# Swapping the order of the first two groups of projected columns in a two-stream hybrid kernel

## The chip, the cores and the metric

The kernel runs on one core of a Trainium2 chip, as one program. The metric is the device time of one execution in microseconds (us).

## The reference

The input is one sequence of 1024 tokens of width 1024, all in float32. Two layers run, each a mixer and an MLP, with RMS norms ahead and residual sums behind:

- Layer 0's mixer projects the normed input to 2560 columns (`h @ w_in`). The first 1792 are shifted (each token mixed with the one before it) and feed eight recurrent heads of 64 (RWKV-7: a state of 64 x 64 per head, updated for every token from r, k, v, a decay and a rate); the other 768 are queries, keys and values of a sliding-window attention. Both results side by side are projected by `w_out`.
- Layer 1's mixer is a gated projection, a causal depthwise convolution of 31 taps, a layer norm, SiLU and a projection.
- The MLP is `square(relu(h @ w1)) @ w2` with 4096 hidden columns.

## The kernel before

The tokens are taken in two halves of 512. Activations lie transposed, 128 columns of the model across the partitions and 512 tokens along them. Each product is made from three matmuls (`mm3`, lines 308 to 310), since both operands are split into a high part and a remainder (`lo`, line 272); weights are loaded in two pieces by SyncE's queue (line 286), cast by ScalarE (line 291), and their remainder is made by VectorE or GpSimd in turn, by a running count.

Layer 0's recurrent heads are worked on in four pairs p = 0 to 3, for each of the two halves `hf`: eight scans (`scan`, lines 571 to 869), each a chunked form of the recurrence with many small matmuls that alternate with vector work. A scan needs the three columns r, k and v of its pair (`rkv(p)` gives their indices, k and v first), which `proj` multiplies out (`w_in_tile`) and shifts (`shift`, `shifted`, lines 545 to 568; the first vector product of a column of half 0 is line 551). It begins on TensorE with the two products of lines 589 and 591, after an activation on k (line 596), and ends with the transposes of line 866 and the vector product of line 869. For half 0 the columns of pairs 0 and 1 stay on the chip; their buffers have the tags krv0 and krv1, by the parity of the column. The columns of pairs 2 and 3 and of half 1 go to memory and are loaded again (lines 945 and 950).

The scans form two streams, A and B, each a serial chain:

```python
def scans_b():
    yield from first1()
    yield from self.scans(1, [(0, 0), (0, 2)])
    self.close(self.cms1)
    self.done.add("b")
...
gs = {"p": params, "A": lambda: self.scans(0, [(0, 1), (0, 3), (1, 0), (1, 1), (1, 2), (1, 3)]), "B": scans_b,
      "n": self.norm0, "0": lambda: att(0), "1": lambda: att(1)}
self.weave(main(), *[gs[c]() for c in ORDER])
```

A pair in the lists is (half, p). A, the longer one, has six scans, B two. B first normalizes and stores the second half (`first1`, transposes of line 355), and its working memory is that of this step.

TensorE's order of instructions is written by a planner (`weave`) when the program is built: it keeps a clock that adds a planned time for TensorE work alone, and takes steps in turn from a base line, `main`, and from the other generators. Each generator names at its `yield` either a planned time after which it is due again (the constants in `LAG`) or a flag that it waits for (`self.done`). Of several due generators the first in `ORDER = "1BAn0p"` is taken, so attention's second part, then B, then A; a ratio limits how much they take from main. The other engines' order is made by the framework from the dependences.

Main is: `cols0` (the columns of half 0; it raises the flags "lg", "0p0" to "0p3" and the attention's), `cols1` (those of half 1), then, behind the flag "b", the output projection of half 0 (`w_out`, which casts the mixers' results in line 1168 and needs the flags "s2", "s3" and "att0" for its parts), the last columns of half 1 and the first half of layer 0's MLP. `scans` waits for "0p1" before A's first scan and for "0p0" before B's; then comes a planned time of `LAG["load"]` and one of `LAG["lora"]` ahead of the first products. Behind the weave come the second half's output projection, its MLP and layer 1.

Of the kernel before, what the change touches and what calls it, by code (L numbers as in the profile page):

```python
# [45 lines left out]
class Net:  # L46
# [1009 lines left out]
    def cols0(self, hs):  # L1056

        self.lg = []
        for j in (12, 13):
            self.lg.append((yield from self.proj(0, hs, j)))  # L1060
        self.done.add("lg")
        self.t = {}
        for p in range(2):
            self.t[p] = []
            for j in self.rkv(p):
                self.t[p].append((yield from self.proj(0, hs, j)))
            self.done.add(f"0p{p}")
        for j in (18, 19, 14, 16, 15, 17):
            yield from self.proj_att(0, hs, j)
            self.done.add(f"0k{j}")  # L1070
        for p in (2, 3):
            js = self.rkv(p)
            for j in js[:1 if p == 3 else 3]:
                yield from self.proj(0, hs, j, True)
            if p == 3:
                pss = yield from self.w_in_pair(js[1:], hs)
                for j, ps in zip(js[1:], pss):
                    self.shift(0, j, ps, True, LAG["hp"] > 0)
            self.done.add(f"0p{p}")
# [525 lines left out]
```

## Time and profile before

| | us |
|---|---|
| three runs: median (lowest, highest) | 2380.85 (2377.12, 2387.97) |
| the profiled execution, its own time | 2379.74 |
| its span, first to last instruction | 2378.0 |
| busy: TensorE / VectorE / ScalarE / GpSimd | 2308.1 / 1532.2 / 1047.7 / 542.8 |
| granted TensorE clock, mean | 0.992 |

The profile's rows give instructions by line of the kernel, with the tiles that they write and read ("out<-in"). PE is TensorE, PEld its weight loads, DVE VectorE, ACT ScalarE, POOL GpSimd, SP SyncE (SPq its queue of loads and stores). Matmuls overlap in the pipeline, so that the durations of neighbours add up to more than the time between their starts.

### The profile page before, as it was taken

To read this page: it belongs to the slowest core of one execution; us is meant where nothing else is said; L and a number is where in the kernel's file an instruction comes from. 1 tells how busy PE (TensorE), PEld (TensorE's weight loads), DVE (VectorE), ACT (ScalarE), POOL (GpSimd) and SP (SyncE) were. 2 spreads that over 40 slices of the span, in tenths; PEclk is the share of its full clock that TensorE was granted. 3 is DMA by queue.
4 is the path that set the end of the run, shared out by engine and by line. 5 is a ranking of instruction groups with operands and counts; after the bars stand their busy time and mean duration, and the time that the engine had idled before them with its cause. 6 is when DMAs were issued, how large, how long until landed. Compare 5 with 4: busy or idle time off the path is not lost.

```text
span 2378.0 us, 38508 instructions
## 1 busy us (share of the span) xinstructions
PE 2308.1 (97%) x14535; PEld 1856.4 (78%) x14535; DVE 1532.2 (64%) x2563; ACT 1047.7 (44%) x1874; POOL 542.8 (23%) x477
## 2 busy tenths in 40 slices
PE   8989889989999999999999999999999999999998
PEld 6767667767777787878888888888878778888887
DVE  7775743667555464569977653799999756533334
ACT  6546634556443332443443363534433544433333
POOL 2322433110111121322000000105555422221121
PEclk9999999999999999999999999999999999999999
DMA  7345234444445454546666665563323333433332
GB/s 219 111 110 153 83 88 132 109 127 123 136 143 178 126 175 133 169 133 200 198 195 191 194 183 172 144 188 98 98 89 98 99 93 94 129 95 98 98 97 85
DMA packets 417934, 320.12 MB, mean 135 GB/s; under 512 B 44642, under 2 KB 360276, under 8 KB 417748
## 3 DMA queue, kind: packets, MB, share of 16 engines
q1 hardware_dynamic: 413684, 309.79, 43.5%
q0 software_dynamic: 2176, 4.19, 0.6%
q10 hardware_dynamic: 1888, 3.67, 0.5%
q8 instruction: 114, 1.87, 0.3%
q14 instruction: 72, 0.59, 0.1%
HBM read 257.29 MB, written 60.29 MB: 134 GB/s over the span
## 4 chain that ended last, share of the span: by engine, by line
PE 75%; DVE 15%; DMA 4%; ACT 3%; issue 2%; SPq 0%; POOL 0%; DVEq 0%; ACTq 0%; POOLq 0%
PE mm L308 23%; PE mm L309 22%; PE mm L310 22%; DVE acc L1321 5%; DMA raw<-p 1%; PE sc L734 1%; DVE C L709 1%; DVE E L711 1%; PE sc L652 1%; DVE hidl L272 1%; PE sc L817 1%; PE sc L771 1%; DMA cx<-d 1%; DVE x L1253 1%; PE at L936 1%
## 5 line engine op out<-in xcount | busy, mean ns | idle before, releaser
L291 ACT CAST whi<-wraw 128x512 fp32r<-128x512 f32 x720 | 445.7, 621 | 986.9 <-PE mm L309 890.9
L308 PE MATMUL mm<-h,whi 128*128 128x512 f32 x1792 | 725.8, 406 | 7.1 <-ACT h L383 2.4
L310 PE MATMUL mm<-h,wlo 128*128 128x512 f32 x1792 | 704.1, 394 | 1.4 <-POOL wlo L272 1.4
L309 PE MATMUL mm<-h,whi 128*128 128x512 f32 x1792 | 703.3, 393 | 1.3 <-DVE h L272 1.0
L272 POOL TENSOR_TENSOR wlo<-wraw,whi 128x512 fp32r<-128x512 f32 x302 | 422.2, 1399 | 1233.8 <-ACT whi L291 1178.5
L1321 DVE SCALAR_TENSOR_TENSOR acc<-u,par,acc 128x512 f32<-128x512 f32 x480 | 429.8, 905 | 10.0
L308 PEld LDWEIGHTS mm<-h,whi 128*128 128x128 f32 x1792 | 339.7, 190 | 89.7 <-issue 12.8
L310 PEld LDWEIGHTS mm<-h,wlo 128*128 128x128 f32 x1792 | 339.1, 189 | 75.7 <-POOL wlo L272 2.3
L309 PEld LDWEIGHTS mm<-h,whi 128*128 128x128 f32 x1792 | 340.0, 190 | 69.0 <-issue 2.4
L308 PE MATMUL mm<-hidh,whi 128*128 128x512 f32 x992 | 389.4, 396 | 0.1
L309 PE MATMUL mm<-hidl,whi 128*128 128x512 f32 x992 | 386.0, 390 | 0.9 <-DVE hidl L272 0.9
L310 PE MATMUL mm<-hidh,wlo 128*128 128x512 f32 x992 | 384.5, 390 | 0.9 <-POOL wlo L272 0.9
L272 DVE TENSOR_TENSOR wlo<-wraw,whi 128x512 fp32r<-128x512 f32 x258 | 183.5, 712 | 200.9 <-ACT whi L291 193.2
L1253 DVE TENSOR_TENSOR x<-mm,x 128x512 f32<-128x512 f32 x248 | 166.5, 686 | 85.9 <-PE mm L310 85.5
L308 PEld LDWEIGHTS mm<-hidh,whi 128*128 128x128 f32 x992 | 186.2, 188 | 43.5 <-issue 4.2
L310 PEld LDWEIGHTS mm<-hidh,wlo 128*128 128x128 f32 x992 | 186.2, 188 | 40.3 <-POOL wlo L272 1.3
L309 PEld LDWEIGHTS mm<-hidl,whi 128*128 128x128 f32 x992 | 186.3, 188 | 40.0 <-DVE hidl L272 1.3
L272 DVE TENSOR_TENSOR hidl<-rel,hidh 128x512 fp32r<-128x512 f32 x109 | 84.9, 780 | 77.9 <-ACT hidh L1230 76.5
L1232 DVE CAST hidh<-rel 128x512 fp32r<-128x512 f32 x68 | 34.2, 506 | 89.8 <-ACT rel L1226 89.6
L1226 ACT ACTIVATE rel<-rel 128x512 f32<-128x512 f32 x128 | 80.6, 633 | 3.9 <-ACT rel L1225 0.4
L1225 ACT ACTIVATE rel<-mm 128x512 f32<-128x512 f32 x128 | 75.6, 593 | 2.2 <-DVE hidl L272 2.0
L1557 POOL COPY u<-u 128x30 f32<-128x30 f32 x8 | 3.2, 399 | 250.2 <-DVE acc L1321 250.2
(377 smaller groups left out, 2191.9 us busy)
## 6 DMA issues: line engine op xcount, KB each, us to landing
wraw<-in_mlp_w_dram SPq DMA_DIRECT2D x512, 256.0 KB
lo<-wlo SPq DMA_DIRECT2D x160, 256.0 KB
wlo<-lo SPq DMA_DIRECT2D x160, 256.0 KB
wraw<-in_cv_pw_w_dram SPq DMA_DIRECT2D x96, 256.0 KB
wraw<-in_hy_w_in_dram SPq DMA_DIRECT2D x80, 256.0 KB
wraw<-in_hy_w_out_dram SPq DMA_DIRECT2D x32, 256.0 KB
p<-stg SPq DMA_DIRECT2D x30, 256.0 KB
raw<-p SPq DMA_DIRECT2D x40, 128.0 KB
```

Source lines behind the costliest of these rows:

```text
L272: return eng.tensor_tensor(out=out, in0=x, in1=hi.bitcast(F32), op=ALU.subtract)
L291: nc.scalar.copy(out=hi, in_=raw)
L308: mm(ps, lhsT=whi, rhs=xhi, start=start, stop=False)
L309: mm(ps, lhsT=whi, rhs=xlo, start=False, stop=False)
L310: return mm(ps, lhsT=wlo, rhs=xhi, start=False, stop=stop)
L652: mm(ps[64 * q:64 * q + 64, u * P:(u + 1) * P], lhsT=src[hs, c * 64:(c + 1) * 64], rhs=ar[hs, :, c, :], start=(u == 0), stop=(u == 3), ski ...
L709: tt(out=j3[:, 0:n, 0:m], in0=a3[:, j, j + 1:16].unsqueeze(2).to_broadcast([64, n, m]), in1=x3[:, j:j + 1, 0:m].to_broadcast([64, n, m]), ...
L1225: nc.scalar.activation(out=t, in_=ps, func=AF.Relu)
L1226: nc.scalar.activation(out=t, in_=t, func=AF.Square)
L1232: nc.vector.tensor_copy(out=hi, in_=t)
L1253: last = nc.vector.tensor_tensor(out=x, in0=pss[o], in1=x, op=ALU.add)
L1321: nc.vector.scalar_tensor_tensor(out=acc, in0=u[:, j:j + H], scalar=self.pv(f"dw{j}", c), in1=acc, op0=ALU.mult, op1=ALU.add)
```

## The change

In `cols0` the loop that projects the columns of pairs 0 and 1 takes pair 1 first. The three columns of pair 1 (A's first scan) stand where those of pair 0 (B's first scan) stood, and the flags "0p1" and "0p0" are raised in this order.

```diff
@@ -1060,7 +1060,7 @@
             self.lg.append((yield from self.proj(0, hs, j)))
         self.done.add("lg")
         self.t = {}
-        for p in range(2):
+        for p in (1, 0):
             self.t[p] = []
             for j in self.rkv(p):
                 self.t[p].append((yield from self.proj(0, hs, j)))
```

## Rows read from the trace of the kernel before

**Rows 1.** The page, busy us, share of the span and instructions by engine

```profile
PE 2308.1 (97%) x14535; PEld 1856.4 (78%) x14535; DVE 1532.2 (64%) x2563; ACT 1047.7 (44%) x1874; POOL 542.8 (23%) x477
```

**Rows 2.** Stretches: from:to, length, each engine's busy us, granted clock, DMA share, GB/s

```profile
core 0: us, PE busy (x) PEld busy (x) DVE busy (x) ACT busy (x) POOL busy (x), PEclk, DMA share, GB/s
...
60.00:160.00 100.00, 86.72 (x792) 67.09 (x790) 76.38 (x190) 50.27 (x98) 29.90 (x28) 0.95 0.41 114
160.00:260.00 100.00, 97.39 (x1202) 73.02 (x1199) 65.76 (x161) 66.49 (x142) 27.64 (x41) 1.00 0.41 118
260.00:360.00 100.00, 86.48 (x1129) 66.60 (x1130) 53.05 (x135) 41.38 (x71) 39.25 (x41) 0.97 0.33 93
360.00:420.00 60.00, 60.00 (x508) 44.89 (x505) 23.43 (x45) 27.91 (x50) 21.66 (x20) 1.00 0.44 135
420.00:560.00 140.00, 131.29 (x1162) 102.04 (x1162) 97.29 (x214) 74.46 (x153) 18.52 (x16) 0.98 0.41 118
560.00:695.00 135.00, 130.84 (x1152) 102.71 (x1149) 78.68 (x193) 62.41 (x129) 19.71 (x17) 0.97 0.42 129
695.00:824.00 129.00, 128.00 (x1081) 100.09 (x1081) 72.02 (x150) 47.77 (x81) 22.27 (x19) 1.00 0.52 159
824.00:953.00 129.00, 127.52 (x1078) 100.17 (x1079) 69.60 (x151) 47.68 (x81) 20.50 (x17) 1.00 0.49 151
...
1100.00:2378.00 1278.00, 1265.41 (x5587) 1042.66 (x5585) 852.34 (x1102) 520.07 (x880) 291.35 (x208) 1.00 0.44 133
```

**Rows 3.** Timeline of PE: start, us; output projection's first, last scan's, MLP half's last product

```profile
411.31 0.40 PE L308 MATMUL mm<-mih,whi 128*128 128x512 f32 x1
...
950.84 0.60 PE L866 MATMUL sc<-ident,BD 128*128 128x128 f32 x4
...
985.77 0.39 PE L310 MATMUL mm<-hidh,wlo 128*128 128x512 f32 x1
```

**Rows 4.** Timeline of PE, first products of scans: B, A, B, A

```profile
64.26 0.69 PE L589 MATMUL sc<-lg,wa 64*128 64x512 f32 x1
...
77.53 0.69 PE L589 MATMUL sc<-lg,wa 64*128 64x512 f32 x1
...
230.25 0.69 PE L589 MATMUL sc<-lg,wa 64*128 64x512 f32 x1
...
259.90 0.69 PE L589 MATMUL sc<-lg,wa 64*128 64x512 f32 x1
```

**Rows 5.** Timeline of DVE, last vector products of the same four scans

```profile
225.46 0.68 DVE L869 TENSOR_TENSOR mi<-mi,BD 128x512 f32<-128x512 f32 x1
...
259.19 1.69 DVE L869 TENSOR_TENSOR mi<-mi,BD 128x512 f32<-128x512 f32 x1
...
379.23 0.69 DVE L869 TENSOR_TENSOR mi<-mi,BD 128x512 f32<-128x512 f32 x1
...
411.72 0.69 DVE L869 TENSOR_TENSOR mi<-mi,BD 128x512 f32<-128x512 f32 x1
```

**Rows 6.** Timeline of DVE, columns: third and sixth of pairs 0 and 1, last of pair 3

```profile
50.21 0.69 DVE L551 TENSOR_TENSOR krv<-mm,rb 128x512 f32<-128x512 f32 x1 [0.21 <-PE mm L310]
...
75.17 0.68 DVE L551 TENSOR_TENSOR krv<-mm,rb 128x512 f32<-128x512 f32 x1
...
219.22 0.68 DVE L551 TENSOR_TENSOR stg<-mm,rb 128x512 f32<-128x512 f32 x1
```

**Rows 7.** Timeline of ACT, B's first activation; in brackets idle before it and its releaser

```profile
65.19 0.72 ACT L596 ACTIVATE BD<-krv,par 128x512 f32<-128x512 f32 x1 [1.79 <-DMA hd<-xl]
```

**Rows 8.** Timeline of ACT, casts ahead of the output projection

```profile
380.01 3.75 ACT L1168 CAST mih<-mi 128x512 fp32r<-128x512 f32 x7 [0.42 <-DVE mi L869]
```

**Rows 9.** Stretches of 5 us inside the second pair of scans, columns as in rows 2

```profile
320.00:325.00 5.00, 1.20 (x31) 1.14 (x32) 1.82 (x4) 0.36 (x1) 0.79 (x1) 0.92 0.77 183
325.00:330.00 5.00, 5.00 (x18) 3.89 (x17) 0.75 (x2) 1.79 (x3) 1.21 (x1) 0.74 0.00 0
```

## Prediction

> **What bounds the kernel now.** I read the page's busy times first, then a table of stretches, then the places of the scans on TensorE in the timeline, then the waits inside the stretch that the edit touches. The page says that TensorE is busy for 97% of the span [rows 1]: what is to be seen is that it is nearly full everywhere, so an edit that neither removes nor adds TensorE work can only change its idle time or its clock. The table of stretches shows where there is any [rows 2]: from 60 to 420 us, where two scans run beside each other, TensorE is idle for 13.28 + 2.61 + 13.52 + 0 = 29.4 us, and the granted clock of 0.95 and 0.97 in two of the stretches takes another (0.05 + 0.03) x 100 = 8 us. From 420 to 695 us, one scan with the second half's attention beside it, it is 8.71 + 4.16 us idle and 0.02 x 140 + 0.03 x 135 = 6.9 us of clock. With one scan alone (695 to 953 us, two scans) only 2.5 us are idle at full clock. So all that the change can touch is a pool of about 37 us up to 420 us and 20 us behind it.
>
> Next, who waits for whom over the long run. Stream A's last scan puts its last transposes on TensorE at 950.84 us; the main line's last product of the first MLP half starts at 985.77 us [rows 3]. Main outlasts A by 35 us. Stream B's end (its last vector product, at 379.23 us) opens the output projection, whose first product starts at 411.31 us [rows 3, 5]: B has 31 us to spare there. Neither stream is the bound; main is, being TensorE itself.
>
> **The change, part by part.** Nothing is removed or added. Six columns are projected in another order; each brings the same 24 products, two weight loads of 256 KB, two casts, two remainders and the same shift work. The choice of engine for a remainder goes by a running count, so the n-th column has the same one as before, and the load queue sees loads of one size in the same places. The two streams' columns go to different buffer tags, so no buffer is reused in another order among the six. Cost of these: 0, and there is no wait in them to uncover.
>
> What moves are the flags. "0p1" rises after the third pair-column instead of the sixth, "0p0" after the sixth instead of the third. In the profile the third column's vector product starts at 50.21 us, the sixth's at 75.17 us [rows 6]. B's first scan starts at 64.26 us, A's at 77.53 us [rows 4]. B was not held by its columns (done at 50.21) but by the second half's normalization, behind which its first activation waits for the store of that half until 65.19 us [rows 7]. A was held by the sixth column. Afterwards A is ready at 50.21 us; I give it the 6 us that the planned load time and first lag take, since B's flag needs such a lag too, so A starts at 56 us: 21.5 us earlier. B takes A's place at the sixth column: 77.5 us, 13.3 us later, past the store, whose wait falls away; it was ScalarE's (1.79 us idle) and hid behind columns on TensorE, so it is worth 0. The two lags between the starts become 21.5 us (was 13.3) in the first pair.
>
> How long a scan lasts, from its first product to the end of its last vector product [rows 4, 5]: leader of the first pair 225.46 + 0.68 - 64.26 = 161.9 us; its follower 259.19 + 1.69 - 77.53 = 183.4; leader of the second pair 379.23 + 0.69 - 230.25 = 149.7; its follower 411.72 + 0.69 - 259.90 = 152.5.
>
> A afterwards: first scan 56 + 161.9 = 218 to 56 + 183.4 = 239 us. Its second needs columns of pair 3, whose last vector product comes at 219.22 us [rows 6]; with the same 6 us that is 225 us at the earliest, so it starts at 225 to 243 and ends at 375 to 396 us, 16 to 37 us earlier than now. All four later scans of A move up by about as much, and main's 35 us of lead become 50 to 70. Main still ends last: worth 0. The group that needs A's second scan in the output projection, now served at 412.4 us with nothing to spare, gets spare time; that it lacked any costs little today, since 360 to 420 us has no idle time at all [rows 2].
>
> B afterwards: first scan 77.5 + 161.9 = 239 to 261 us, second start 239 to 265 (now 4 us behind the end of the first), end 389 to 417.5 us. The output projection needs a cast (3.75 / 7 = 0.54 us [rows 8]) and a remainder behind that, so about 1.3 us: B must end by 410.0. The cost is 0 for most of this interval and 7.5 us at its end. Queued behind this flag is all of main, and A's third scan alone could fill TensorE. I take 1 us: the middle of the interval (403) is in time.
>
> The stalls of the two pairs cannot be read for offsets that did not run. The offsets were 13.3 us with 13.28 + 2.61 + 5 = 20.9 us lost, and 29.7 us with 13.52 + 3 = 16.5 us lost [rows 2, 4]. They become 21.5 and, from the ends above, about 14 to 22. Both lie between the two that ran, so both are put at the mean, 18.7: 2 x 18.7 = 37.4, as now, change 0. From below, each of the four scans could stall as little as a scan alone, 1.2 us: 4.8 instead of 37.4, a gain of 32. From above, both offsets at or under that of the first pair: 2 x 20.9 = 41.8, +4, and more only by the rival below. Behind 420 us A's third and fourth scan meet the second half's attention in another phase; of 20 us lost there I assume as much as now, with -15 to +15 for the unknown.
>
> Sum: 0 + 0 + 1 + 0 = +1 us on the profiled execution of 2379.7 us (span 2378.0 and 1.7 around it). It lies 1.1 us under the median of 2380.85, so 2382 us.
>
> One rule speaks against reading TensorE as full. The row is the 97% of [rows 1]; the weight loads of [rows 2] are busy for 251.6 of 360 us from 60 to 420 (70%) and 1042.7 of 1278 from 1100 on (82%). The Trainium skill (Perfetto Trace Analysis, Identifying the Most-Contended Engine) holds that the busy share of matmuls misjudges headroom and that the share of weight loads is the better measure. By that, up to 360 - 251.6 / 0.816 = 52 us could be had in this stretch, against 37 by idle time and clock. I stay with the idle time: the scans' weight loads are smaller ones, so that their share is lower even in a full stretch, and the edit does not create work to fill what is hidden.
>
> **The rivals.** Slower: B becomes the late one. It is now the follower in both pairs, and the follower of the first pair lost 183.4 - 161.9 = 21.5 us. For it: 320 to 330 us shows how one late step holds all of TensorE, 3.8 us idle and then a granted clock of 0.74 [rows 9]. Against it: the planner asks B ahead of A, and the second follower lost only 2.8 us. If B's first scan takes 183.4 us, its second starts at 265, and main waits for 265 + x + 1.3 - 411.3 = x - 145 us, x being its second scan. It decides from x = 157 us on (over 12 us, which is 0.5%); at x = 167, midway between the two followers, it is +22: 2403 us.
>
> Faster: the pairs interleave better. A's first scan begins in a stretch that has no idle time, and B no longer runs through the start together with it; if the first pair loses what two lone scans lose, 2.5 us instead of 20.9, that is -18: 2363 us. For it: most of the pool is there. Against it: two scans still run together with the first half's attention, whose VectorE work sets much of these waits (76 of 100 us busy from 60 to 160 [rows 2]).
>
> Nothing happens: both streams have so much to spare that only their order is swapped, and each loss is found again elsewhere: 2381 us. It is hardly to be told from the forecast and is counted with it.
>
> **How the numbers follow.** 0.5% is 12 us, about what a measurement here tells from no change. Forecast and "nothing happens" together 0.58. Slower 0.25: 0.15 by B, 0.10 by new meetings of A's later scans with the attention (+15). Faster 0.17: 0.12 by the first pair, 0.05 by the later meetings or by the headroom of the rule. The range reaches to both rivals' prices, 2362 to 2403, with about 0.09 left out on either side; the likeliest case alone has 2370 to 2393.
>
> **What would show it.** Right: first scan products at about 56 and 77.5 us, A's; A's second scan begun by 243 us and its last one ended 16 to 37 us earlier; the output projection's first product at 408 to 414 us; the end of the first MLP half within 8 us of 986; idle time from 60 to 420 us within 8 us of 29. Wrong: a stretch without main's products ahead of the output projection (B late), or over 12 us of the idle time of the pairs gone or added, or the changed order moving time behind 990 us, where I see nothing that it could reach.

## The result, and the profile after

The changed kernel takes 2397.69 us (median of six, 2392.44 to 2403.76), the kernel before 2379.36 us: a ratio of 1.0078 with a 95% interval of 1.0061 to 1.0095. It is slower by 0.8%: inside the range, but above the 2393 us to which the likeliest case alone reached. The profiled execution took 2392.44 us with a span of 2390.7 us, 12.7 us longer than before; it is the shortest of the six, so it shows the loss at its smallest.

The page's engine row of the changed kernel, to be read beside [rows 1]: the same instructions on TensorE.

```profile
PE 2317.9 (97%) x14535; PEld 1860.3 (78%) x14535; DVE 1534.2 (64%) x2563; ACT 1046.3 (44%) x1874; POOL 541.1 (23%) x477
```

Its stretches, as in [rows 2]:

```profile
60.00:160.00 100.00, 84.90 (x753) 65.50 (x753) 74.51 (x183) 46.28 (x87) 27.90 (x28) 0.91 0.41 112
160.00:260.00 100.00, 93.67 (x1101) 68.56 (x1099) 53.93 (x127) 54.44 (x114) 25.00 (x37) 0.95 0.39 115
260.00:360.00 100.00, 88.74 (x1164) 69.21 (x1164) 63.42 (x166) 50.80 (x99) 38.33 (x39) 0.95 0.33 91
360.00:420.00 60.00, 60.00 (x561) 45.10 (x561) 22.82 (x51) 26.71 (x47) 22.29 (x22) 1.00 0.37 112
420.00:560.00 140.00, 133.66 (x1131) 103.77 (x1131) 91.37 (x196) 70.48 (x143) 22.97 (x19) 0.94 0.42 123
560.00:695.00 135.00, 130.61 (x1186) 101.31 (x1185) 82.70 (x205) 66.70 (x143) 19.83 (x17) 0.99 0.43 131
```

From 60 to 420 us TensorE is idle for 15.10 + 6.33 + 11.26 + 0 = 32.7 us, 3 more than before. The column of the granted clock is what moved: 0.91, 0.95 and 0.95 take 19 us where 0.95, 1.00 and 0.97 took 8, and 420 to 560 us has 0.94 where it had 0.98.

The places of the scans and of main in the timeline of TensorE, as in [rows 3, 4]: the four first scans, the output projection's first product, the last scan's transposes, the MLP half's last product.

```profile
58.66 0.69 PE L589 MATMUL sc<-lg,wa 64*128 64x512 f32 x1
...
80.58 0.90 PE L589 MATMUL sc<-lg,wa 64*128 64x512 f32 x1
...
246.00 1.12 PE L589 MATMUL sc<-lg,wa 64*128 64x512 f32 x2
...
253.06 1.22 PE L589 MATMUL sc<-lg,wa 64*128 64x512 f32 x1
...
421.41 0.39 PE L308 MATMUL mm<-mih,whi 128*128 128x512 f32 x1
...
962.84 0.60 PE L866 MATMUL sc<-ident,BD 128*128 128x128 f32 x4
...
1000.21 0.39 PE L310 MATMUL mm<-hidh,wlo 128*128 128x512 f32 x1
```

The last vector products of the same four scans, as in [rows 5]:

```profile
244.14 0.68 DVE L869 TENSOR_TENSOR mi<-mi,BD 128x512 f32<-128x512 f32 x1
...
252.90 0.67 DVE L869 TENSOR_TENSOR mi<-mi,BD 128x512 f32<-128x512 f32 x1
...
397.08 0.69 DVE L869 TENSOR_TENSOR mi<-mi,BD 128x512 f32<-128x512 f32 x1
...
420.45 1.78 DVE L869 TENSOR_TENSOR mi<-mi,BD 128x512 f32<-128x512 f32 x1
```

A starts first (58.66 us) and B second (80.58), 21.9 us apart. But the second scans start 7.1 us apart, and by the order that the planner wrote B's is the first of them. A's lead is gone, and its last scan ends 12 us later than before instead of earlier. Up to the output projection 10.1 us are lost (421.41 against 411.31), from there to the end of the MLP half another 4.3 (1000.21 - 985.77 = 14.4), and behind it 1.7 us come back.

One stretch shows how the clock carries the loss: TensorE of the changed kernel behind 495 us, in stretches of 5 us, and the product that waited there.

```profile
495.00:500.00 5.00, 1.78 (x128) 1.78 (x128) 5.00 (x7) 4.33 (x10) 1.71 (x1) 0.74 0.54 183
500.00:505.00 5.00, 5.00 (x53) 3.64 (x44) 3.14 (x7) 1.14 (x2) 0.00 (x0) 0.50 0.83 238
505.00:510.00 5.00, 3.81 (x39) 2.60 (x38) 1.81 (x3) 1.60 (x3) 0.00 (x0) 0.50 0.16 37
510.00:515.00 5.00, 5.00 (x14) 3.92 (x13) 1.80 (x3) 0.98 (x2) 0.00 (x0) 0.56 0.55 172
515.00:520.00 5.00, 5.00 (x46) 3.90 (x44) 3.15 (x5) 3.35 (x6) 0.00 (x0) 1.00 0.21 61
```

```profile
498.22 1.08 PE L734 MATMUL sc<-BD,E 32*32 32x32 f32 x64 [3.23 <-ACT BD L740]
```

A scan's product waits 3.23 us for a copy on ScalarE; then TensorE, though nearly always busy, runs at 1.2 GHz (granted 0.50) until about 514 us. Beside the 3.2 us of waiting the clock takes 5 x (0.26 + 0.50 + 0.50 + 0.44) = 8.5 us.

The kernel before has waits of this length at the same line as well, one at the same time and one, for the same copy, from 145 to 148 us. Each is shown with the stretches around it, the granted clock being the third number from the end:

```profile
498.20 0.27 PE L734 MATMUL sc<-E,F 32*32 32x32 f32 x2 [3.02 <-ACT F L750]
```

```profile
495.00:500.00 5.00, 1.46 (x34) 1.08 (x33) 1.80 (x3) 2.20 (x4) 0.00 (x0) 0.83 0.41 124
500.00:505.00 5.00, 5.00 (x13) 3.94 (x13) 2.92 (x5) 1.51 (x3) 0.00 (x0) 0.50 0.50 160
505.00:510.00 5.00, 5.00 (x49) 3.95 (x48) 3.34 (x7) 2.53 (x4) 1.30 (x1) 0.99 0.33 106
```

```profile
148.08 0.72 PE L734 MATMUL sc<-BD,E 32*32 32x32 f32 x62 [3.24 <-ACT BD L740]
```

```profile
105.00:156.00 51.00, 42.93 (x510) 33.82 (x506) 41.02 (x124) 22.28 (x51) 14.54 (x14) 1.00 0.44 115
```

Behind the first the clock is back at 505 us and has taken 3.4 us; behind the second it does not fall at all (granted 1.00 from 105 to 156 us). So waits of 3.0 to 3.2 us cost 0, 3.4 and 8.5 us of clock, and their length alone does not tell which.

### The profile page after: what moved, and what is told of

Same layout as the page of the kernel before. It is cut to its first block, busy times and chain, and to the rows that moved or that the text cites. A ratio compares the mean times of both kernels' runs of the same rounds, so it can differ in the third digit from the quotient of the medians.

```text
span 2390.7 us, 38505 instructions
## 1 busy us (share of the span) xinstructions
PE 2317.9 (97%) x14535; PEld 1860.3 (78%) x14535; DVE 1534.2 (64%) x2563; ACT 1046.3 (44%) x1874; POOL 541.1 (23%) x477
## 4 chain that ended last, share of the span: by engine, by line
PE 79%; DVE 13%; ACT 3%; issue 2%; DMA 2%; SPq 0%; POOL 0%; DVEq 0%; ACTq 0%; POOLq 0%
PE mm L308 24%; PE mm L309 23%; PE mm L310 23%; DVE acc L1321 5%; PE sc L734 1%; PE sc L652 1%; DVE h L272 1%; DMA raw<-p 1%; DVE hidl L272 1%; PE sc L771 1%; DVE x L1253 1%; PE sc L817 1%; DVE nt L517 1%; PE at L936 1%; DVE wlo L272 1%
```

## One account for all kernels

Everything from 16 us to the end of the MLP half is the same 8421 matmuls on TensorE in every kernel of this study. The rows of that stretch, first before, then changed:

```profile
16.00:986.20 970.20, 923.89 (x8421) 718.28 (x8422) 590.71 (x1336) 464.83 (x886) 218.57 (x218) 0.98 0.45 135
```

```profile
16.00:1000.60 984.60, 935.46 (x8421) 723.53 (x8422) 594.10 (x1334) 463.49 (x885) 216.78 (x218) 0.97 0.45 133
```

Idle time is length less busy time. The clock's loss is the sum of (1 - granted) over stretches of 1 us, finer than the two digits of the rows. What is left is the time the work takes without either.

| kernel | ratio to before (95%) | length | idle | clock | left |
|---|---|---|---|---|---|
| before | 1 | 970.2 | 46.3 | 17.1 | 906.8 |
| changed | 1.0078 (1.0061 to 1.0095) | 984.6 | 49.1 | 34.1 | 901.4 |
| e1 | 1.0110 (1.0095 to 1.0125) | 995.1 | 60.3 | 32.4 | 902.4 |
| e2 | 1.0056 (1.0040 to 1.0072) | 985.7 | 52.3 | 29.0 | 904.4 |
| e3 | 1.0075 (1.0056 to 1.0095) | 987.6 | 50.7 | 30.7 | 906.2 |
| e4 | 1.0025 (1.0015 to 1.0036) | 972.0 | 43.8 | 17.1 | 911.1 |
| f1 | 1.0067 (1.0054 to 1.0080) | 989.0 | 54.0 | 34.1 | 900.9 |
| f2 | 1.0049 (1.0036 to 1.0062) | 983.5 | 51.5 | 25.6 | 906.4 |
| f3 | 1.0068 (1.0053 to 1.0084) | 989.1 | 54.5 | 29.0 | 905.6 |
| f4 | 1.0039 (1.0025 to 1.0053) | 980.9 | 48.2 | 32.4 | 900.3 |
| g1 | 0.9947 (0.9935 to 0.9959) | 958.0 | 37.0 | 15.4 | 905.6 |
| g2 | 1.0037 (1.0026 to 1.0049) | 982.0 | 48.1 | 32.4 | 901.5 |
| g3 | 1.0100 (1.0085 to 1.0115) | 992.2 | 56.3 | 32.4 | 903.5 |
| h1 | 0.9965 (0.9951 to 0.9978) | 960.1 | 39.4 | 17.1 | 903.6 |

The last column holds within 11 us while the lengths differ by 37. So what the change lost in this stretch is waiting and the clock behind it, not more work or a worse mixture of it. The two columns are not to be added up to the us: of the 14.4 us by which the stretch grows, 2.8 are idle time and 11.6 busy time of the same matmuls, while the clock's column grows by 17. It also counts lowered clock while TensorE is idle (6.8 us of idle time in the changed kernel, 1.1 us before), and there nothing more is lost.

The table stands on one execution of each kernel. Over all six executions of the changed kernel, span times one less the mean granted clock is 34 to 41 us, 37 in the mean; over the 44 of the kernel before that were timed beside the experiments it is 17 to 31, 22 in the mean. By this the clock is up to 15 of the 19 us between the mean spans. Where in a kernel a loss falls is less certain: e1 below differs from the changed kernel only from A's second scan on, and yet it waits or loses to the clock 35.5 us from 60 to 246 us where the changed kernel has 30.1. Differences of some 5 us in one place prove little.

## The experiments

Planned times are the planner's own clock, which counts TensorE's work alone. Each kernel was timed beside the kernel before. Each theory is stated in the expected text in which its number first comes up.

**e1, A's second scan held** (the changed kernel):

```diff
+            if (hf, p) == (0, 3):
+                yield 25.0
             yield from self.scan(hf, p, r, k, v, self.lg[0], ...
```

> The changed kernel, but A's second scan is held back by 25 planned us, so that the second pair of scans starts about 28 planned us apart (B first) instead of 3; its first pair stays as changed. Theory 1 (the loss comes from the second pair starting together, as A lost its lead to B's precedence and to the late columns of pair 3): most of the 18 us comes back, 2378 to 2387 us, the granted clock of 250 to 360 us rises from about 0.94 to 0.97 or more. Theory 2 (the loss comes from the first pair, where A leads but is taken after B): it stays at 2393 to 2402 us. Theory 3 (any departure from the constants' tuning costs as much): 2393 us or more.

Measured 2405.64 us. The second scans start 41 us apart (251.5 and 292.3 us), and nothing comes back: theory 1 falls as the main cause. The time lies above theory 2's range and in theory 3's.

**e2, B's second scan held** (the kernel before):

```diff
+            if (hf, p) == (0, 2):
+                yield 26.0
```

> The kernel before, with its column order, but B's second scan is held back by 26 planned us, so that the second pair starts 2.5 planned us apart instead of 27; its first pair stays. Theory 1: 10 to 18 us slower than before, 2389 to 2398 us, with a lower clock between 230 and 360 us. Theory 2: as before, within 5 us of 2379. Theory 3: slower by an amount that has nothing to do with the place, 2385 to 2400 us.

Measured 2393.46 us, the size that theory 1 gave, but not in its place: of the 18 us more that it waits or loses to the clock, only 3 lie from 250 to 350 us and 13 lie behind, up to 550 us, where A's later scan meets the second half's attention. Theory 2 misses; theory 3 had this size, too.

**e3, B's first scan held** (the kernel before):

```diff
+            if (hf, p) == (0, 0):
+                yield 13.0
```

> The kernel before, but B's first scan is held back by 13 planned us: the first pair then starts 3 planned us apart (58 and 55) instead of 12, the second pair 21 apart. This is B's delay without A's early start. Theory 1: the second pair is apart, so at most the first pair's own meeting costs, 2379 to 2388 us. Theory 2: as A does not lead, 2375 to 2384 us. Theory 3: slower by 10 us or more.

Measured 2395.08 us. B's delay alone, with A where it was, costs as much as the whole change. Theories 1 and 2 had it near 2380 us: both miss. Theory 3 had 10 us or more. On the chip A starts at 75.4 us here and B at 78.7, so that A leads by 3 us and is asked behind B.

**e4, A asked ahead of B** (the changed kernel):

```diff
-ORDER = "1BAn0p"
+ORDER = "1ABn0p"
```

> The changed kernel, but the planner asks A ahead of B, so that A keeps its lead: planned starts 39 and 58, second scans 181 (A) and 210 (B), B ends later by 23 planned us. Theory 1: the second pair is 29 apart, so the loss goes: 2374 to 2386 us. Theory 2: the first pair's order of precedence is the cause, so the loss goes as well, 2374 to 2386 us. Theory 3: slower than before by 10 us or more. The rival of the prediction (B late for the output projection): a stretch without main's products ahead of it, 2390 us or more.

Measured 2383.57 us: one letter's place takes some 13 of the 18 us back (1.0078 to 1.0025), and theory 3 as a law falls. Theories 1 and 2 both had this time, so that the run does not tell them apart. The first scans start where they do in the changed kernel (58.00 and 80.89 us), but A keeps its lead (second scans at 226.73 and 267.16 us). B is now late for the output projection, whose first product moves to 428 us, yet the MLP half ends only 1.8 us later than before: of the 30 us from 400 to 430 TensorE is busy for 27.4, for A's work is pulled forward (its third scan starts at 391 us where it started at 419). That is the rival "B becomes the late one", under its own price: B ends at 419.8 us, for which its formula gives 10 us.

```profile
16.00:988.00 972.00, 928.18 (x8421) 719.15 (x8422) 589.45 (x1335) 468.41 (x888) 218.04 (x218) 0.98 0.45 135
```

**f1, the mirror**, the same exchange in the kernel before:

```diff
-ORDER = "1BAn0p"
+ORDER = "1ABn0p"
```

> The mirror: the kernel before, with its column order (B leads by 12 planned us), but the planner asks A ahead of B. Planned: first scans 45 (B) and 57 (A), second scans 193 (B) and 196 (A), so that the leader loses its lead. Theory 4 (what costs is a leader that is asked behind its follower; the changed kernel has this, and with A ahead in turn it was gone): 8 to 20 us slower than before, 2386 to 2398 us, with the loss in the granted clock of 60 to 350 us. Theory 3 (any departure costs): the same number, so this run alone does not tell the two apart. Theory 5 (A asked first is the better order whatever the columns do): 2370 to 2380 us.

Measured 2393.5 us, and the loss lies where theory 4 put it: from 60 to 350 us this kernel waits or loses to the clock 53.1 us, the kernel before 37.9 (and the changed kernel 51.5). With e4 this makes a square: the leader asked first gives 2379 (B leads) and 2384 us (A leads), the leader asked behind its follower 2393.5 and 2397.7 (leader: of the first pair). Theory 5 falls; neither the columns nor the letters are bad by themselves, their combination is.

**f2, A's first scan held** (the changed kernel):

```diff
+            if (hf, p) == (0, 1):
+                yield 18.0
```

> The changed kernel, but A's first scan is held by 18 planned us: both first scans start together (55 and 58), the second ones at 185 (B) and 217 (A). All later planned times are those of before to 4 us; what is left of the change is B's delay of 10 planned us and the columns' order. Theory 4: A no longer leads, so 2376 to 2385 us. Theory 6 (the first pair's meeting costs where the two scans stand closer than in the kernel before or are led by A, since the constants fit one offset only): as with B held in the kernel before, 2390 to 2402 us.

Measured 2389.57 us, between the two. From 60 to 350 us it waits and loses to the clock 35.6 us, where the kernel before has 37.9; its loss lies at 411 to 550 us, 10.6 us idle and 13.7 of clock (before 7.8 and 3.4). Theory 4 (2376 to 2385 us) misses, and theory 6 (2390 to 2402) does by half a us.

**f3 and f4, more planned time on every lag**:

```diff
-SLACK=0.306
+SLACK=0.6
```

> The changed kernel with the planner's extra time on each lag at 0.6 instead of 0.306 us, so that each step of scans and attention is placed a little later on TensorE; the planned end of the weave moves by 3.5 us. Theory 6 (the new meetings make steps come later than their lags allow, TensorE waits for them, and each such wait is followed by a lower clock): idle time and clock loss up to 1000 us fall by 8 us or more, 2382 to 2391 us. If the lags are not the cause: 2398 to 2404 us, the planned 3.5 us more.

> The control: the kernel before with the same extra time of 0.6 us; its planned end moves by 1 us. Theory 6: the lags fit here already, so little is to be had: 2374 to 2384 us. If longer lags lose as any departure does (theory 3): 2388 us or more.

Measured 2396.72 us for the changed kernel, no difference, and 2387.69 us for the kernel before, 9 us slower. Longer lags don't mend it, so that theory 6 falls in this form; and the loss of f4 comes with B leading and asked first in both pairs, as before; the second pair starts 41 us apart where it had 30. Both times lie outside what theory 6 gave; f4's is near theory 3's 2388.

**g1 and g2, a shorter solve in each scan** (before and changed):

```diff
-        for j in range(15):
+        for j in range(3):
```

> The kernel before with the 15 steps of each scan's small solve cut to 3 (the other 12 pairs of vector operations are left out, so the scans' results are not the reference's). TensorE's instructions and their order stay exactly those of the kernel before; only the vector chain between them is shorter, by some 5 to 10 us of VectorE in each scan. Both theories: somewhat faster than before, 2360 to 2378 us, since its waits at the products behind the solve shrink.

> The changed kernel with the same cut, TensorE's order exactly that of the changed kernel. Theory 7 (what the change costs are waits of TensorE for the vector chains of scans that meet, and the lower clock behind them): with the chains shorter most of the difference to the kernel before goes; this run minus the one of the kernel before with the same cut is 0 to 8 us, not 18. Theory 8 (it is TensorE's order itself, its small and large products in another mixture, or the output projection's later place): the difference stays 14 to 22 us.

Measured 2367.49 and 2387.46 us: both gain, 12 and 10 us, and their difference stays at 20 us. The vector chain of the solve is not what the change costs, and theory 7 falls for the solve; the rest of the scans' vector work was left as it was. Theory 8 has its number. The mixture of products is not the reason, for g2's stretch has 901.5 us of work left as the others have, and 28 us more of waiting and clock than g1's; that the order on TensorE decides which waits arise is not excluded by it.

**g3, A ahead of B only in the first pair** (A ahead as in e4, and in the planner's `first`):

```diff
-ORDER = "1BAn0p"
+ORDER = "1ABn0p"
...
         def first(ds):
+            if ds is due and "s1" in self.done:
+                ds = [d for d in due if d[1] is gens[2]] + [d for d in due if d[1] is not gens[2]]
```

> The changed kernel, with A asked ahead of B only until A's first scan has ended, and B ahead of A from then on. The first pair is as with A in turn throughout; in the second one A leads by 21 planned us and is asked behind B, and B ends early enough for the output projection (planned 342 instead of 348). Theory 4 (a leader asked behind its follower costs in either pair): 2389 to 2400 us. If only the first pair matters: 2376 to 2385 us, at or under the run with A ahead throughout.

Measured 2402.23 us, the worst but one: a leader asked behind its follower costs in the second pair as well, as theory 4 says (it had 2389 to 2400 us). It isn't clean, since B stands ahead of the attention too from there on.

**h1, the attention without its softmax** (the changed kernel; lines 901 to 919 go, and the masks get harmless fills):

```diff
-            nc.vector.tensor_reduce(out=m2(0), in_=sc, axis=AX.X, op=ALU.max)
...
-                    act(out=sc[:, n, h, :], in_=sc[:, n, h, :], func=AF.Exp, scale=0.125, bias=ms[:, 1, c:c + 1],
-                        accum_out=ms[:, 2, c:c + 1])
...
-                act(out=sc[:, n, 0, :], in_=sc[:, n, 0, :], func=AF.Copy, scale=ms[:, 4, c:c + 1])
```

> The changed kernel, with the vector work of the attention's softmax left out (maximum, exponentials, sums and scaling; the masks are replaced by finite numbers, so the output is not the reference's). The scores go straight to the transposes. TensorE's instructions and their order in the weave stay those of the changed kernel; VectorE and ScalarE have less to do beside the scans of both halves, and the attention's own steps are early. Theory 9 (the change costs by scans and attention meeting on VectorE and ScalarE: attention steps come late, and make scan steps late): 2376 to 2388 us, most of the difference gone, with fewer and shorter stretches of lower clock up to 550 us. If the scans alone make the waits: 2391 us or more.

Measured 2369.36 us: 28 us under the changed kernel, with TensorE's order in the weave unchanged and less work beside it in the stretch: ScalarE is busy for 408 us where it was 463, VectorE for 554 where it was 594.

```profile
16.00:976.10 960.10, 920.72 (x8421) 715.96 (x8422) 553.85 (x1208) 408.24 (x702) 216.03 (x218) 0.98 0.46 137
```

The waits of TensorE from 60 to 420 us are, at the top, first changed, then h1 (line numbers are 1 and 20 lower there):

```profile
PE at L894 <- ACT asc L928: 7.1, 2, 6.2
PE sc L652 <- DVE ar L622: 5.4, 3, 2.6
PE sc L734 <- DVE F L751: 5.3, 2, 5.0
PE sc L591 <- ACT BD L867: 2.7, 1, 2.7
PE sc L734 <- ACT F L750: 2.6, 2, 1.6
```

```profile
PE sc L652 <- DVE ar L622: 7.1, 2, 5.2
PE at L893 <- ACT asc L908: 4.3, 1, 4.3
PE at L893 <- DVE asc L898: 3.2, 1, 3.2
PE sc L617 <- ACT F L609: 2.5, 3, 1.1
PE mm L308 <- ACT stg L563: 1.1, 1, 1.1
```

The waits that go are the scans', at line 734 (5.3 and 2.6 us) and line 591 (2.7 us). The attention's own stay (7.1 us, and 4.3 + 3.2 in h1), and one of the scans' grows, 5.4 to 7.1 us. So without the softmax some steps of the changed kernel's scans come in time. But the kernel before, softmax and all, waits at line 734 as long in this stretch:

```profile
PE sc L734 <- DVE F L751: 3.9, 1, 3.9
...
PE sc L734 <- ACT BD L740: 3.2, 1, 3.2
...
PE sc L734 <- DVE C L743: 1.6, 1, 1.6
```

The waits at line 734 are therefore not what the change added (that at line 591 is new), and theory 9 is not shown. Its own range, 2376 to 2388 us, was missed from below: more came back than the change costs. What the same cut would give the kernel before was not run, so how much of the 28 us belongs to the change stays open; the kernel before has 63.4 us of idle time and clock in all, h1 56.5.

No order tried was faster than the kernel before with the whole work done.

## Why the prediction was right or wrong

Right were the parts that could be counted. The six columns cost nothing themselves. The first scans start at 58.66 and 80.58 us (said: 56 and 77.5). TensorE's idle time from 60 to 420 us is 32.7 us (said: within 8 of 29). Main ends the weave, with 37 us of lead over A (said: 50 to 70). No stretch without main's products stands ahead of the output projection. Behind the MLP half nothing is lost (2390.7 - 1000.6 = 1390.1 us, before 2378.0 - 986.2 = 1391.8).

Wrong was first the step "A afterwards": its second scan was to start at 225 to 243 and end at 375 to 396 us, and it starts at 253 and ends at 422. A's first scan takes 244.14 + 0.68 - 58.66 = 186.2 us, longer than the longer of the two that had been read, because the planner asks B ahead of it as soon as B runs; with A asked first (e4) it takes 159.9 us. The prediction knew this rule and used it only to defend B. So the offset of the second pair came out at 7.1 us and not at 14 to 22, under both that had run, and A's last scan moved back by 12 us. Three of the prediction's signs fail with it: A's second scan begun by 243 us, the output projection's first product by 414 us (421.4) and the MLP half's end within 8 us of 986 (1000.6).

Wrong was, above all, the step "The stalls of the two pairs": it put the change of stalls at 0 by a mean of the two offsets read. Its idle time was right, its clock was not. The clock's loss up to 420 us went from 8 to 19 us, and up to 1000 us it doubled, 17.1 to 34.1. In the step's own sum the two pairs lose 32.7 + 19 = 51.7 us where they lost 37.4, so the term was +14 and not 0, and its upper bound (+4) was too low by far. The step took the loss of a pair, clock included, for a matter of its offset alone; the waits of 3 us above, with 0, 3.4 and 8.5 us of clock behind them, show that the clock's part does not follow from the waits' length either. Behind 420 us, where up to 15 us were allowed, lie 4.3 us. Of the 12.7 us between the two profiled executions, 10.1 lie up to the output projection, 4.3 between there and the end of the MLP half, and 1.7 come back; the rest of the 18 us between the medians is the distance of the profiled execution from its median, 5.3 us below it in the changed kernel, 0.4 us above it (2379.74 against 2379.36) in the kernel before.

The rivals: "B becomes the late one" did not happen in the changed kernel (B ends at 397.8 us, in time), and where it did, in e4, the whole kernel is 6 us slower than before. (Midway between the two followers is 168 and not 167 us, which moves that rival's price by 1 us.) "The pairs interleave better" did not happen; of the waits that it put down to the attention's VectorE work, the trace of the kernel before names that work as releaser for only 2.8 of 29 us. The headroom of 52 us worked out from the share of weight loads was found by no order. What happened is what the prediction cited for its slower rival, 3.8 us idle and then a lowered clock [rows 9], in more places.

That the time fell inside the range is in good part luck. The upper end, 2403 us, was the price of B coming late, which did not come. The other slower case, new meetings of A's later scans with the attention at +15 us, comes nearest in size, but it put its loss behind 420 us, where 4.3 us of it lie.

On the clock the traces agree with the Trainium skill (TensorE: Matmul & The Clock Gate, HAM oscillation): gaps between bursts of matmuls throttle the array, and the price is paid anew each time. The records hold 8 stretches of lowered clock before 1000 us in the kernel before and 12 in the changed one, and 19 of these 20 begin in a wait of TensorE of 1.4 us or more or within 2.5 us behind one. But not every wait has its price: none follows those of 3.2 us at 145 and 2.8 us at 296 us in the kernel before, nor that of 2.6 us at 100 us in the changed one.

Shown are the account (the loss is waiting and mostly clock), the four times of the square of e4 and f1 (with the first pair's leader asked first 0 and 6 us are lost, with it asked behind its follower 15 and 18), and that the solve's chain is not the carrier. Not shown is that the softmax beside the scans is. Only argued is why the orders of e2, e3, f2 and f4 cost 0.4 to 0.75% each although the leader is asked first or leads by 3 us only (e3, behind its follower). Their losses beyond those of the kernel before lie in different places: e2's and f2's mostly behind 350 us (13 us each), e3's up to 350 us (18), f4's up to 250 us (13) and from 411 to 550 us (8). No run separates the meetings of scans and attention there from each other. So a weaker form of theory 3 stays open beside theory 4: the planner's constants fit the order of the kernel before, and every other order pays 5 us or more.

## What to carry to other kernels

Where several streams share an engine whose order is fixed ahead, a stream that is made ready earlier keeps no lead unless the rule of precedence lets it go ahead; look up who is asked first before moving a start. Price a wait of TensorE by its idle time and by the stretch of lower clock that follows; together these stretches were the larger part here, though behind a single wait of 3 us they took anything from 0 to 8.5 us. Offsets between streams that run well are found by trial: of the nine other orders and lags tried with the whole work done, none was better, and interpolating between two known offsets gave the wrong size.

## What was not expected of the hardware

A wait of 3.2 us on TensorE was followed by about 17 us at half clock although TensorE was busy in most of that time (rows from 495 to 515 us). With the shorter solve (g2) the same stretch loses 8.5 us again (granted 0.53, 0.50, 0.50 and 0.77 from 495 to 515 us), so it is no chance of one execution. The kernel before waited there for 3.0 us and had its clock back after about 7 us. ScalarE's loads of function tables (1.28 us each), which the meeting of two scans seemed likely to multiply, did not: 31 up to 680 us in both kernels.
